# Down products of an encoder block by seven quarter products, with casting and adding transfers for their weights

## The chip, the cores and the metric

The kernel runs on one core of one Trainium2 chip. The metric is the device time of one execution in microseconds (us), as the median of several runs. The profile is that of one further execution. Engines are named as the profile names them: PE (TensorE, matmul), DVE (VectorE), ACT (ScalarE), POOL (GpSimd), SP (SyncE, which issues most transfers here).

## The reference, cut to what matters

One layer over 512 tokens of width 1024: a half-step SwiGLU (FFN1), a mixing part (convolution and gated linear attention), a second half-step SwiGLU (FFN2), a gated input embedding, a final norm. Everything is float32. The change is in the two SwiGLUs:

```python
D_MODEL = 1024; SEQ = 512; D_FF = 2816
def _swiglu(x, w_in, w_out):
    gate, up = jnp.split(x @ w_in, 2, axis=-1)
    return (jax.nn.silu(gate) * up) @ w_out

h = h + 0.5 * _swiglu(_rmsnorm(h, ffn1_norm[i]), ffn1_w_in[i], ffn1_w_out[i])
...
h = h + 0.5 * _swiglu(_rmsnorm(h, ffn2_norm[i]), ffn2_w_in[i], ffn2_w_out[i])
```

## The kernel before

**Number format.** Each float32 operand is split into a high part (a rounding copy to fp32r, on ACT: `high`, `split`) and a low part (operand minus high part, on DVE: `low`). A product is then three matmuls: high by high, low by high, high by low. A weight tile is 128 x 1024 (512 KB), so its split is one ACT cast and one DVE subtraction of 1024 elements per partition. `added` makes the low part without DVE: ACT writes minus the source (rounded) into it, and a POOL transfer adds the source.

**Gate and up.** The 2816 hidden columns are 22 blocks of 128, taken two at a time: 11 pairs. Most pairs are computed by seven quarter products (a Strassen-Winograd scheme) called m1 to m7, each of 24 matmuls with 256 moving columns. The weights' sums s1 to s4 are made by DVE (`s12`, `s3_`, `s4_`); the activations' t1 to t4 once per FFN. Some early pairs are "plain": eight units h0 to h7 of twelve 512-column matmuls. FFN1 has pairs 1 and 2 plain, FFN2 pair 1. After its products, a pair's results pass PSUM, an ACT copy (`snap`, into `sq` or `u2`), DVE additions and scalings (`plus`, `times_row`, `gated`) and an ACT Silu, and become the activations `m`; `act_parts` splits these into `actH` and `actL`.

**Down.** `CUTS` collects blocks into groups of four (the last of two). `second` computes a group as four pieces (two column halves e, two token halves th). A piece of a four-block group is 24 matmuls of 512 columns in two PSUM banks of its own; DVE then adds each bank, scaled, to the running sum `hall` (a SCALAR_TENSOR_TENSOR, called an eviction here). So a group takes 96 matmuls and 8 evictions. Its weights come as four raw 512 KB tiles, cast by ACT and subtracted by DVE.

**Order.** `drive` walks a list of units. A unit has jobs that are issued some units ahead (`AHEAD = 4`; fetches 7 or 9), then what the unit before left over (`left`, for instance the Silu), then its matmuls and evictions. `Ordered` makes PE, DVE and ACT run strictly in the order in which the instructions were issued, so an instruction that waits holds up all that stands behind it on its engine. A pair i runs m6, m7, m5 of pair i, m1 and m2 of pair i+1, m4, m3 of pair i, with pieces of the down product after m2 and after m3. Transfers issued by SP wait in SP's queue for a free buffer; `raw` has 6 buffers for weight tiles and `sm` two for sums.

Of the kernel before, what the change touches and what calls it, by code (L numbers as in the profile page):

```python
# [29 lines left out]
D_PLE = 256  # L30
EPS = 1e-6
HALF = SEQ // 2
CUTS = ((0, 4), (4, 8), (8, 12), (12, 16), (16, 20), (20, 22))


# [27 lines left out]
def block_kernel(ctx: ExitStack, tc: tile.TileContext, a: dict, out: bass.AP):  # L63
# [16 lines left out]
    def nm(s):  # L80
        uid[0] += 1
        return f"{s}_{uid[0]}"

    NA = 41
    NCV = 4

    def bt(dt=F32, s="a"):
        return big.tile([P, SEQ], dt, tag="A", bufs=NA, name=nm(s))

# [79 lines left out]
        return hi, lo  # L169

    def raw(nk, ncol):
        return wp.tile([P, 1024], F32, tag="raw", bufs=6, name=nm("wr"))[:, :nk * ncol].rearrange(
            "p (k c) -> p k c", k=nk)

    def fetch(r3, src, k0, nk, c0, ncol):
# [210 lines left out]
    class Left:  # L386
# [12 lines left out]
            dve.tensor_tensor(out=out, in0=x, in1=y, op=op)  # L399

        def tile(self):
            return wp.tile([P, 1024], F32, tag="sm", bufs=2, name=nm("sm")).rearrange("p (k c) -> p k c", k=4)

        def part(self, name, engine=None):

# [9 lines left out]
        def s12(self):  # L415
            if hasattr(self, "s1"):
                return
            self.s1, self.s2 = self.tile(), self.tile()
            self.sum(self.s1, self.a21, self.a22, ALU.add)
            self.sum(self.s2, self.s1, self.a11)  # L420

        def s3_(self):
            if hasattr(self, "s3"):
# [15 lines left out]
    def h_of(t, e):  # L439
        return hall[:, t, e * SEQ:(e + 1) * SEQ]  # L440
# [187 lines left out]
        for f in left:  # L628
            f()

    def ffn(w_in, w_out, x, nxt, given, first, rs_of, rsb, hooks, plain):


        got = {}
# [40 lines left out]
        def gated(p, s, u, i):  # L675
            if not hasattr(p, "m"):
                p.m = tmp("m", 2 * SEQ, bufs=1).rearrange("p (f c) -> p f c", f=2)
            dve.tensor_tensor(out=p.m[:, :, i * HALF:(i + 1) * HALF], in0=two(u), in1=two(s), op=ALU.mult)

        def act_parts(p):  # L680
            c = [c for c, (f0, f1) in enumerate(CUTS) if f0 <= p.f < f1][0]
            to = cvt if c % 2 == 0 and p.f == CUTS[c][0] else bt
            p.acts = [split(p.m[:, f, :], "act", to) for f in range(2)]
# [14 lines left out]

        def m6(p):
            mul(p.x, p.part("s2"), x.op["t2"], False, False)  # L700
            p.u2 = snap(p.x, "u2", bufs=1)

        def m7(p):
            p.w = bank()
# [41 lines left out]
        def unit(kind, i):  # L746
            p = pairs[i]

            def go(run):
                left = run(p)  # L750
                hooks.get((kind, i), lambda *_: None)()
                return left

            if kind[0] == "h":
                j = int(kind[1])
                part, run = (f"a{1 + j // 4}{1 + j % 2}", plain_unit(j)) if j % 4 < 2 else (None, plain_unit(j))
                if part:
                    return [(AHEAD, lambda: p.part(part)), (9, lambda: p.fetch(part))], lambda: go(run)
            else:
                part, run = USES[kind]  # L760
            before = [(AHEAD + (kind == 'm5'), lambda: p.part(part))] if part else []
            if kind in ("m1", "m2"):
                before.append((7, lambda: p.fetch(part)))
            elif kind == "m6":
                before += [(9, lambda: p.fetch("a21", "a22")), (6, p.s12)]
            elif kind in ("m7", "m3"):
                before.append((6, p.s3_ if kind == "m7" else p.s4_))

            return before, lambda: go(run)

        def second(cut):

            f0, f1 = cut
            kn = f1 - f0
            last = f1 == CUTS[-1][1]

# [33 lines left out]
                units.insert(3, ([], lambda: nxt.half(0)))  # L810
            return units

        units, had = [], set()
# [18 lines left out]
        for i in range(start, npair):  # L832
            add("m6", i)
# [12 lines left out]
            due = due[2:]  # L846
            if i in cut_of and i < end:
                due += second(cut_of[i])
        units += due + second(CUTS[-1])

        p0 = pairs[0]
# [26 lines left out]
    hooks = sums_hooks(xb, ("t2", "t3", "t1", "t4"), (("h5", 1), ("h7", 1), ("h3", 2), ("m1", 3)))  # L878
# [589 lines left out]
    def quarter(to, k, e, tag="raw", bufs=6):  # L1468
# [47 lines left out]
        sub(q11[jp], q12[jp], q11[jp])  # L1516

    def second_sum(jp):
        t2.append(narrow("sm", 2, "sm"))
        sub(t2[jp], q11[jp], q22[jp])  # L1520

    def third_sum(jp):
# [8 lines left out]
    def todo(*fs):  # L1531
        return lambda *_: [f(*v) for f, *v in fs]

    hooks.update({("d16", 1): todo((act.activation, warm, ones, AF.Sigmoid), (quarter, q11, 0, 0), (quarter, q21, 1, 0, "sm", 2), (quarter, q12, 0, 1)),
                  ("d16", 2): todo((q_high, b11, q11, 0), (quarter, q22, 1, 1), (project_in,)),
                  ("d16", 3): todo((q_high, b11, q11, 1)),
                  ("d20", 0): todo((q_high, b21, q21, 0), (first_sum, 0), (third_sum, 0)),
# [4 lines left out]
    nxt = Turn("ple_norm", xp)  # L1542
    nxt.hg = hg
    rs2_ = mid
    ffn(ffn2_in, a["ffn2_w_out"][0], xb, nxt, wf, ((g0, u0), (g1_, u1_)), lambda: rs2_[0], mid[1], hooks, (1,))

# [256 lines left out]
```

## Time and profile before

| | us |
|---|---|
| median of 3 runs (lowest to highest) | 961.56 (959.86 to 962.09) |
| the profiled execution | 960.76 |
| its span, first to last instruction | 959.0 |
| PE busy | 943.4 |
| DVE busy | 723.6 |
| ACT busy | 472.1 |
| POOL busy | 55.9 |

Rows of a timeline are start and duration in us, engine, line, operation, output<-inputs; a bracket tells how long the engine was idle before and what released it. All recorded operations carry line 46, the recording helper, so tiles tell operations apart: `wr` raw weights, `wh` and `wl` their parts, `sm` the sums s1 and s2, `hall` an eviction, `g`, `s`, `u`, `m` the steps to the activations.

### The profile page before, as it was taken

How to read it: one execution, taken by the hardware profiler on the slowest of the kernel's cores; microseconds unless marked ns; L12 is line 12 of the kernel's file. 1: busy time of each engine (PE TensorE's matmuls, PEld its weight loads, DVE VectorE, ACT ScalarE, POOL GpSimd, SP SyncE). 2: the span in 40 equal slices, each digit the busy share in tenths (PEclk: the TensorE clock that was granted, in tenths of full speed). 3: DMA queues.
4: the chain of work that ended last, by engine and by line, in shares of the span. 5: the costliest groups of instructions: out<-in, count | busy, mean ns of one | idle time of the engine just before them, and what ended most of it. 6: DMA issues, size and time to landing. Idle time of an engine off the chain costs nothing.

```text
span 959.0 us, 14433 instructions
## 1 busy us (share of the span) xinstructions
PE 943.4 (98%) x5810; PEld 832.5 (87%) x5810; DVE 723.6 (75%) x975; ACT 472.1 (49%) x721; POOL 55.9 (6%) x71
## 2 busy tenths in 40 slices
PE   9999999999999999999999999999999999999896
PEld 7888999999999988788878889999999999998674
DVE  5776877878787666999987467777777778766796
ACT  5552544334443465463566654344433443354983
POOL 0000200000000110001210010000000000001211
PEclk9999999999999999999999999999999999999998
DMA  7541223243224493255563471432233322454643
GB/s 226 178 137 62 89 90 126 71 132 110 89 70 130 138 240 85 69 130 133 133 149 98 105 176 44 133 110 89 91 108 110 113 98 77 154 198 114 116 81 107
DMA packets 90214, 112.88 MB, mean 118 GB/s; under 512 B 5075, under 2 KB 65669, under 8 KB 90148
## 3 DMA queue, kind: packets, MB, share of 16 engines
q1 hardware_dynamic: 84260, 94.67, 31.1%
q0 software_dynamic: 5872, 17.30, 9.9%
q8 instruction: 45, 0.74, 0.3%
q14 instruction: 21, 0.17, 0.1%
q10 hardware_dynamic: 16, 0.00, 0.0%
HBM read 93.61 MB, written 2.10 MB: 100 GB/s over the span
## 4 chain that ended last, share of the span: by engine, by line
PE 95%; ACT 2%; DVE 1%; DMA 0%; issue 0%; POOL 0%; POOLq 0%; SPq 0%; ACTq 0%; DVEq 0%
PE ps L46 94%; PE ax L46 1%; ACT wh L46 1%; DMA wr<-in_ffn_w_in 0%; ACT sq L46 0%; DVE s L46 0%; DVE g L46 0%; ACT hgH L46 0%; DVE rs L46 0%; DVE y L46 0%; ACT wl L46 0%; DVE wl L46 0%; POOL rs L46 0%; ACT wq L46 0%; POOLq L1801 0%
## 5 line engine op out<-in xcount | busy, mean ns | idle before, releaser
L46 PE MATMUL ps<-hgH,wh 128*128 128x256 f32 (+1 forms) x768 | 238.9, 316 | 0.2 <-DVE wh L46 0.2
L46 PE MATMUL ps<-hgL,wh 128*128 128x256 f32 (+1 forms) x768 | 237.7, 315 | 0.0
L46 PE MATMUL ps<-hgH,wl 128*128 128x256 f32 (+1 forms) x768 | 237.3, 314 | 0.0
L46 DVE TENSOR_TENSOR wl<-wr,wh 128x1024 fp32r<-128x1024 f32 (+1 forms) x158 | 188.7, 1208 | 63.2 <-ACT wh L46 63.1
L46 ACT CAST wh<-wr 128x1024 fp32r<-128x1024 f32 (+1 forms) x172 | 176.6, 1041 | 75.3 <-PE ps L46 46.5
L46 PEld LDWEIGHTS ps<-hgH,wh 128*128 128x128 f32 x768 | 146.7, 191 | 11.3 <-issue 1.1
L46 PEld LDWEIGHTS ps<-hgL,wh 128*128 128x128 f32 x768 | 146.1, 191 | 9.6 <-DVE hgL L46 0.3
L46 PEld LDWEIGHTS ps<-hgH,wl 128*128 128x128 f32 x768 | 146.4, 191 | 8.8
L46 PE MATMUL ps<-wh,actH 128*128 128x512 f32 x352 | 137.6, 391 | 0.0
L46 PE MATMUL ps<-wh,actL 128*128 128x512 f32 x352 | 137.3, 390 | 0.0
L46 PE MATMUL ps<-wl,actH 128*128 128x512 f32 x352 | 137.0, 389 | 0.0
L46 ACT ACTIVATE s<-g 128x512 f32<-128x512 f32 x48 | 30.4, 633 | 156.3 <-DVE g L46 156.3
L46 DVE SCALAR_TENSOR_TENSOR hall<-ps,rsh,hall 128x512 f32<-128x512 f32 x96 | 71.1, 748 | 29.3 <-PE ps L46 28.3
L46 DVE SCALAR_TENSOR_TENSOR cv<-glu,cw,cv 128x502 f32<-128x502 f32 (+24 forms) x120 | 81.1, 732 | 0.6
L46 PEld LDWEIGHTS ps<-wl,actH 128*128 128x128 f32 x352 | 66.1, 188 | 14.0
L46 PEld LDWEIGHTS ps<-wh,actH 128*128 128x128 f32 x352 | 66.2, 188 | 12.9
L46 PEld LDWEIGHTS ps<-wh,actL 128*128 128x128 f32 x352 | 66.2, 188 | 12.4
L46 ACT CAST wh<-sm 128x1024 fp32r<-128x1024 f32 x38 | 39.8, 1047 | 41.4 <-DVE sm L46 35.6
L46 DVE TENSOR_TENSOR wl<-sm,wh 128x1024 fp32r<-128x1024 f32 x38 | 46.3, 1222 | 4.3 <-ACT wh L46 3.9
L46 ACT COPY sq<-ps 128x512 f32<-128x512 f32 x38 | 22.3, 587 | 54.5 <-PE ps L46 54.5
L46 DVE TENSOR_TENSOR sm<-wr,wr 128x1024 f32<-128x1024 f32 x17 | 21.0, 1236 | 28.9 <-DMA wr<-in_ffn_w_in 28.9
L46 ACT CAST actH<-m 128x512 fp32r<-128x512 f32 x44 | 25.6, 619 | 31.9 <-DVE m L46 31.9
(251 smaller groups left out, 1684.1 us busy)
## 6 DMA issues: line engine op xcount, KB each, us to landing
wr<-in_ffn_w_in SPq DMA_DIRECT2D x84, 512.0 KB
wr<-in_ffn_w_out SPq DMA_DIRECT2D x44, 512.0 KB
wr<-in_w_in SPq DMA_DIRECT2D x20, 512.0 KB
wl<-wr POOLq DMA_DIRECT2D x15, 512.0 KB, 5.4
wr<-in_w_out SPq DMA_DIRECT2D x8, 512.0 KB
wq<-in_ple_w_gate SPq DMA_DIRECT2D x8, 512.0 KB
wl<-wq POOLq DMA_DIRECT2D x8, 512.0 KB, 4.6
wa<-wr POOLq DMA_DIRECT2D x12, 256.0 KB, 6.6
```

The lines of the kernel that those rows point to most:

```text
L46: inst = call(*args, **kwargs)
```

## The change

It makes four groups per FFN (blocks 4 to 20, `Q1` and `Q2`) by a new `second_quarters`; the first and the last group keep the four pieces. The two layers of the short description are the two FFNs. FFN1's pair 2 is done by m1 to m7 and no longer plain.

The activations of a group are held as quarters a11, a12, a21, a22 (two blocks by 256 tokens), its weights as b11, b12, b21, b22 (two blocks by 512 columns). Seven products, called q0 to q6 here in their order (j = 0 to 6), replace the four pieces:

| | operands | PSUM banks |
|---|---|---|
| q0 | a12 by b21 | y |
| q1 | a11 by b11 | x |
| q2 | s2 by t2 | x, added |
| q3 | s1 by t1 | x, added |
| q4 | s4 by b22 | x, added |
| q5 | s3 by t3 | w |
| q6 | a22 by t4 | w, added |

Each has 12 matmuls of 512 columns into two banks, and each is followed by two evictions of what the banks then hold. Products q1 to q4 add into the same two banks that are evicted in between, q6 into those of q5. All of b21, b11 and b22 as used by q0, q1 and q4 come straight from the input array by a casting POOL transfer (`ask`); their low parts by ACT (minus the high part) and an adding POOL transfer (`rest`). The four tiles for t1 to t4 are also loaded raw, summed by DVE, and split by `added`. DVE also makes the activations' s1 to s4, and `act_split` splits seven operands of 128 x 512 where `act_parts` split four.

```diff
-    NA = 41
+    NA = 38
+    NRAW = 10
...
+        def act_split(g, name):
+            hi, lo = two(bt(F32R, name + "H")), two(bt(F32R, name + "L"))
+            act.copy(hi, g[name])
+            sub(lo, g[name], hi.bitcast(F32))
+            g[name + "p"] = hi, lo
...
+            def ask(name, k, e):
+                w[name] = [wp.tile([P, 1024], F32R, tag=t, bufs=6, name=nm(t)).rearrange("p (k c) -> p k c", k=2)
+                           for t in ("wh", "wl")]
+                pool.dma_start(out=w[name][0], in_=src(k, e))
+            def rest(name, k, e):
+                hi, lo = w[name]
+                act.mul(lo, hi.bitcast(F32), -1.0)
+                pool.dma_start(out=lo, in_=src(k, e).bitcast(F32R), accum_op=ALU.add)
...
+            def product(key, x, y, first, last, th, e, j):
+                def run():
+                    if first:
+                        ps[key] = [bank(), bank()]
+                    wh, wl = w.pop(y)
+                    xh, xl = g.pop(x + "p")
+                    for i in range(2):
+                        ts, o = slice(i * P, (i + 1) * P), ps[key][i]
+                        for k in range(2):
+                            pe.matmul(o, xh[:, k, ts], wh[:, k], start=(first and k == 0), stop=False, skip_group_check=True)
+                            pe.matmul(o, xl[:, k, ts], wh[:, k], start=False, stop=False, skip_group_check=True)
+                            pe.matmul(o, xh[:, k, ts], wl[:, k], start=False, stop=(last and k == 1), skip_group_check=True)
+                        t = 2 * th + i
+                        h = h_of(t, e)
+                        dve.scalar_tensor_tensor(out=h, in0=o, scalar=got["rsh"][:, t:t + 1], in1=h,
+                                                 op0=ALU.mult, op1=ALU.add)
+                    hooks.get((f"d{f0}", {1: 1, 3: 2, 5: 3}.get(j)), lambda *_: None)()
+                    return []
+                return run
+            def direct(name, k, e):
+                return [(AHEAD + 2, lambda: ask(name, k, e)), (AHEAD, lambda: rest(name, k, e))]
+            jobs = [direct("b21", 1, 0) + left(("a12", None)),
+                    direct("b11d", 0, 0) + left(("a11", None)),
+                    [(AHEAD + 3, lambda: (get("b11", 0, 0), get("b12", 0, 1), get("b22", 1, 1))),
+                     (AHEAD + 2, lambda: sums("t1")), (AHEAD + 1, lambda: sums("t3", "t2")),
+                     (AHEAD, lambda: make("t2", "b22"))] + left((None, s3), ("s2", s2)),
+                    [(AHEAD, lambda: make("t1", "b11"))] + left(("s1", s1)),
+                    direct("b22d", 1, 1) + left(("s4", s4)),
+                    [(AHEAD, lambda: make("t3", "b12"))] + left(("s3", None)),
+                    [(AHEAD + 3, lambda: get("b21", 1, 0)), (AHEAD + 1, lambda: sums("t4")),
+                     (AHEAD, lambda: make("t4", "b21"))] + left(("a22", None))]
...
-        for i in range(start, npair):
+        quota = {}
+        for i in range(start, npair):
+            if i not in quota:
+                quota[i], quota[i + 1] = (len(due) + 1) // 2, len(due) // 2
+            at = {0: (), 1: "b", 2: "bd", 3: "abd", 4: "abcd"}[min(quota[i], 4)]
             add("m6", i)
             add("m7", i)
+            place("a")
             add("m5", i)
-            if i == end:
-                units += due[:1]
-                due = due[1:]
-            else:
-                add("m1", i + 1)
+            add("m1", i + 1)
             add("m2", i + 1)
-            units += due[:1]
+            place("b")
             add("m4", i)
+            place("c")
             add("m3", i)
-            units += due[1:2]
-            due = due[2:]
+            place("d")
...
-        (ps0[:2], ps0[2:]), lambda: rs1[0], lambda: spread(rs1[0]), hooks, (1, 2))
+        (ps0[:2], ps0[2:]), lambda: rs1[0], lambda: spread(rs1[0]), hooks, (1,), Q1)
```

`left(...)` puts an operand's sum and split two units ahead of its product. With the quotas, a group's products stand over two pairs. In the first pair: m6 m7 q0 m5 m1 m2 q1 m4 q2 m3 q3. In the second: m6 m7 q4 m5 m1 m2 q5 m4 m3 q6. The fourth group comes due at the last pair, which has no next pair: m6 m7 q0 m5 q1 m4 q2 m3 q3 q4 q5 q6, and then the pieces of the last two blocks. The two sums buffers `sm` are given up; sums and raw tiles share ten `raw` buffers. Work of the next stage that was hooked to pieces 1, 2 and 3 of the group at block 16 is hooked to q1, q3 and q5 now.

More of the change, by code (lines that the diff above doesn't have):

```diff
@@ L629, in drive, with ffn @@
             f()
-    def ffn(w_in, w_out, x, nxt, given, first, rs_of, rsb, hooks, plain):
+    def ffn(w_in, w_out, x, nxt, given, first, rs_of, rsb, hooks, plain, quarters):
         got = {}
@@ L675, in gated @@
         def gated(p, s, u, i):
+            if p.f - p.f % 4 in quarters:
+                g = groups.setdefault(p.f - p.f % 4, {})
+                m = g[f"a{i + 1}{1 + p.f // 2 % 2}"] = two(bt(s="m"))
+                dve.tensor_tensor(out=m, in0=two(u), in1=two(s), op=ALU.mult)
+                return
             if not hasattr(p, "m"):
@@ L811, in second, with second_quarters, src, get @@
             return units
+        def second_quarters(f0):
+            raws, w, g, ps = {}, {}, groups.setdefault(f0, {}), {}
+            def src(k, e):
+                return w_out[(f0 + 2 * k) * P:(f0 + 2 * k + 2) * P, e * SEQ:(e + 1) * SEQ].rearrange("(k p) c -> p k c", p=P)
+            def get(name, k, e):
+                raws[name] = raw(2, SEQ)
+                nc.sync.dma_start(out=raws[name], in_=src(k, e))
+            def ask(name, k, e):
[6 more added lines that the diff above has]
+                pool.dma_start(out=lo, in_=src(k, e).bitcast(F32R), accum_op=ALU.add)
+            def sums(*names):
+                for t, out_, x, y in (("t1", "b11", "b12", "b11"), ("t3", "b12", "b22", "b12"),
+                                      ("t2", "b22", "b22", "b11"), ("t4", "b21", "b21", "b22")):
+                    if t in names:
+                        sub(raws[out_], raws[x], raws[y])
+            def make(name, of):
+                w[name] = added(high(raws[of]))[:2]
+            def left(*todo):
+                def run():
+                    for name, sum_ in todo:
+                        if sum_:
+                            sum_()
+                        if name:
+                            act_split(g, name)
+                return [(2, run)]
+            def s3():
+                sub(g["a11"], g["a11"], g["a21"])
+                g["s3"] = g["a11"]
+            def s2():
+                g["s2"] = two(bt(s="s2"))
+                sub(g["s2"], g["a22"], g["s3"])
+            def s1():
+                dve.tensor_tensor(out=g["a21"], in0=g["a21"], in1=g["a22"], op=ALU.add)
+                g["s1"] = g["a21"]
+            def s4():
+                sub(g["a12"], g["a12"], g["s2"])
+                g["s4"] = g["a12"]
+            def product(key, x, y, first, last, th, e, j):
+                def run():
+                    if first:
[27 more added lines that the diff above has]
+                     (AHEAD, lambda: make("t4", "b21"))] + left(("a22", None))]
+            runs = [product(*v, j) for j, v in enumerate((
[4 rows of a table added]
+            return list(zip(jobs, runs))
@@ L1518, in second_sum @@
     def second_sum(jp):
[L1519 removed]
+        t2.append(narrow("raw", NRAW, "sm"))
         sub(t2[jp], q11[jp], q22[jp])
```

29 lines of the change are left out of this document (21 added, 8 removed), and 4 rows, old and new, of the table runs.

## The prediction

> **What bounds the kernel now.** I read the page first (busy shares, then the chain that ended last), then the matmul's pace on the timeline, then DVE's work and waits in one FFN.
>
> ```profile
> PE 943.4 (98%) x5810; PEld 832.5 (87%) x5810; DVE 723.6 (75%) x975; ACT 472.1 (49%) x721; POOL 55.9 (6%) x71
> ...
> PE 95%; ACT 2%; DVE 1%; DMA 0%; issue 0%; POOL 0%; POOLq 0%; SPq 0%; ACTq 0%; DVEq 0%
> ```
>
> PE sets the time: it is busy for 98% of the span, and the last chain runs on it for 95%. So a matmul taken away is time won, as long as nothing else makes PE wait. How much one is worth stands in the starts, not in the durations (0.28 and 0.39 us, which overlap):
>
> ```profile
> 300.03 0.28 PE L46 MATMUL ps<-hgH,wh 128*128 128x256 f32 x1
> 300.14 0.28 PE L46 MATMUL ps<-hgL,wh 128*128 128x256 f32 x1
> ...
> 305.78 0.40 PE L46 MATMUL ps<-wh,actH 128*128 128x512 f32 x1
> 306.02 0.40 PE L46 MATMUL ps<-wh,actL 128*128 128x512 f32 x1
> ...
> 311.25 0.28 PE L46 MATMUL ps<-t2H,wh 128*128 128x256 f32 x1
> ```
>
> Between 300.03 and 305.78 stand 48 matmuls of 256 columns: 0.12 us each. Between 305.78 and 311.25 stand 24 of 512 columns: 0.228 us each. A product m1 to m7 (24 narrow) takes 2.88 us, a plain unit or a quarter product q (12 wide) 2.73 us.
>
> The second question is how near DVE is to PE in the FFNs. The next rows are the window of FFN2's loop (PE, PEld, DVE, ACT and POOL busy, then clock and transfers) and DVE's waits in it:
>
> ```profile
> 592.00:842.00 250.00, 250.00 (x1742) 234.66 (x1741) 192.03 (x212) 105.41 (x132) 0.00 (x0) 1.00 0.32 105
> ```
> ```profile
> DVE wl L46 <- ACT wh L46: 29.5, 29, 2.0
> DVE sm L46 <- DMA wr<-in_ffn_w_in: 17.2, 8, 3.5
> DVE u L46 <- ACT sq L46: 8.6, 7, 1.3
> ```
>
> PE never stops in 250 us. DVE is busy for 77% of them and idles in small waits, since it works ahead. That is the cover that the change spends.
>
> **The change: what it takes from PE.** A group goes from 96 to 84 wide matmuls. Eight groups: 8 x 12 x 0.228 = 21.9 us. FFN1's pair 2 goes from 96 wide (21.9) to 168 narrow ones (20.2): 1.7 us. Together 23.5 us, if PE never waits.
>
> **What it adds to DVE.** DVE's paces, from starts of neighbours on its timeline:
>
> ```profile
> 640.49 1.22 DVE L46 TENSOR_TENSOR wl<-sm,wh 128x1024 fp32r<-128x1024 f32 x1
> 641.62 0.69 DVE L46 TENSOR_TENSOR g<-ps,sq 128x512 f32<-128x512 f32 x1
> 642.35 0.69 DVE L46 TENSOR_TENSOR g<-g,bc 128x512 f32<-128x512 f32 x1
> 642.95 0.75 DVE L46 SCALAR_TENSOR_TENSOR hall<-ps,rsh,hall 128x512 f32<-128x512 f32 x1
> ...
> 650.47 0.68 DVE L46 TENSOR_TENSOR g<-ps,bc 128x512 f32<-128x512 f32 x1
> ...
> 653.94 0.69 DVE L46 TENSOR_TENSOR m<-u,s 128x512 f32<-128x512 f32 x1
> 654.54 1.54 DVE L46 SCALAR_TENSOR_TENSOR hall<-ps,rsh,hall 128x512 f32<-128x512 f32 x2
> 656.00 1.28 DVE L46 TENSOR_TENSOR actL<-m,actH 128x512 fp32r<-128x512 f32 x2
> ...
> 664.58 0.69 DVE L46 TENSOR_TENSOR u<-ps,sq 128x512 f32<-128x512 f32 x1 [1.26 <-ACT sq L46]
> 667.05 1.23 DVE L46 TENSOR_TENSOR sm<-wr,wr 128x1024 f32<-128x1024 f32 x1 [1.78 <-DMA wr<-in_ffn_w_in]
> 668.31 1.22 DVE L46 TENSOR_TENSOR sm<-sm,wr 128x1024 f32<-128x1024 f32 x1
> 669.45 1.22 DVE L46 TENSOR_TENSOR wl<-wr,wh 128x1024 fp32r<-128x1024 f32 x1
> ```
> ```profile
> 651.19 0.63 ACT L46 ACTIVATE s<-g 128x512 f32<-128x512 f32 x1 [3.22 <-DVE g L46]
> 651.73 1.03 ACT L46 CAST wh<-wr 128x1024 fp32r<-128x1024 f32 x1
> 654.66 1.15 ACT L46 CAST actH<-m 128x512 fp32r<-128x512 f32 x2 [1.89 <-DVE m L46]
> ...
> 663.96 0.59 ACT L46 COPY sq<-ps 128x512 f32<-128x512 f32 x1 [1.90 <-PE ps L46]
> ```
>
> A long operation (1024 elements) holds DVE for 1.14 us (668.31 to 669.45), for 1.26 if the next needs its result (667.05 to 668.31). A short one takes 0.61 (642.35 to 642.95), or 0.73 if the next needs it. Two evictions take 1.4 (654.54 to 656.00). A sum whose split follows at once costs a trip over ACT: sum to cast 0.72 (653.94 to 654.66), cast 0.6, so 1.33 until the low part starts. From m5's last matmul to `u` it is 0.65 (663.96 to 664.58 and a little). From `g` to the end of the Silu it is 1.35 (650.47 to 651.19, and 0.63).
>
> Over two pairs, with one group, DVE has before: 26 long, 18 short, 8 evictions, 46 us of PE's 62.2 (336 narrow and 96 wide). After: 26 long again (the four low parts saved are the four sums t1 to t4), 25 short (four sums and three more low parts), 14 evictions. That is 30.1 + 15.9 + 9.8 = 55.8 us with the dependent ones at their price, and five trips over ACT add 3.6: 59.4. PE would need 40.3 + 84 x 0.228 = 59.4. DVE has no slack left on average, and its queue is in order, so the local chains decide.
>
> **Three stalls in each two pairs.** I laid DVE's queue end to end against PE's units, in the order in which the built program issues them. Wherever DVE must wait for PE and then has more to do before PE's next need than PE has work, PE stops, every time.
>
> *Into q5.* m5 ends; `u` starts 0.65 later, since it needs the copy of m5. Behind it on DVE: `u` 0.61, two sums of weights 1.26 each, s4 of the weights 1.14, t4 1.14, a low part 1.14, the low part of the activations' s3 0.69. That is 7.9 us. PE has m1 and m2, 5.76, and one matmul of q5 that needs only the high part, 0.23. Stall 1.9 us.
>
> *Into q2.* It adds into the banks of q1, so q1's eviction must be over. From q0's end: its second eviction 0.7, t3, t2 and a low part 3.4, `u` and the low part of a11 1.2, two sums 2.5, s4 and a low part 2.3, s3 of the weights 1.14, s3 of the activations 0.73, s2 with its trip 1.33, its low part 0.61, `g` twice 1.34, q1's first eviction 0.75: 16.0 us. PE has m5, m1, m2, q1, m4: 14.25. Stall 1.8.
>
> *Into q3.* From q2's start (q1's first eviction is done): second eviction 0.67, a low part 1.14, `u` and `m` 1.34, a low part 1.14, s1 with its trip 1.33, its low part 0.61, q2's first eviction 0.75: 7.0 us. PE has q2 and m3: 5.6. Stall 1.4.
>
> The same reckoning leaves q4 (8.4 of 8.5 us) and q6 (6.8 of 8.5) just free. Sum 5.1 us: two pairs take 64.5 us instead of 62.2. Each FFN has three such cycles: 6 x 5.1 = 30.6 us.
>
> **The fourth group.** In the last pair q3 to q6 stand back to back. q4 needs the eviction of q3, and before it on DVE from q3's start: an eviction 0.67, s4 with its trip and low part 1.94, `g` and Silu 1.35, a weight cast behind the Silu on ACT 1.0 and its low part 1.14, another low part 0.61, `m` 0.61, the eviction 0.75: 8.1 us where PE has q3, 2.7. Stall 5.3; in FFN2 I take 4.8, since DVE arrives 0.6 earlier. In FFN1 the next stage's weights (eight ACT operations of some 0.6 us, twice, from the hooks at m4 and q3) stand ahead of s1's and a22's casts: I add 1.5 into q3 and 2.2 into q6, in FFN2 0.4. Sum 14 us. Before, the pieces had banks of their own, and nobody waited.
>
> **What I cost at nothing.** Loads: tiles t1 to t4 are asked for only a unit before their first use, but SP may issue as soon as a buffer is free, and with ten buffers the tile that held it was done six units (17 us) earlier or more; before, some had one or two units, the 17.2 us of waits above. If the cover is gone, these waits come back, at most 2.1 us a pair. The casting POOL transfer does not occur before. Its nearest rows:
>
> ```profile
> wl<-wr POOLq DMA_DIRECT2D x15, 512.0 KB, 5.4
> ...
> sm<-in_ple_w_gate POOLq DMA_DIRECT2D x2, 512.0 KB, 7.6
> ```
>
> At 5.4 to 7.6 us it lands in time: `rest` on ACT comes two units (5.6 us) after the issue, and behind it wait first a Silu whose result is due a product later. I take 0; the upper end is 2 us for each of 24 transfers on ACT's queue, 48 us with all of it passed on, and I let a third of it count in the range. FFN1's early part has DVE near PE's pace for ten units (about 33 us of each): 0 taken, 3 at most.
>
> [...]
>
> **Sum.** -23.5 + 30.6 + 14 = +21.1 us on the profiled execution's 960.76 us (span 959.0 and 1.8 around it): 981.9. The median of the runs shown lies 0.8 higher, so 983 us.
>
> **Rivals.**
> *All hidden.* DVE and ACT keep ahead of PE and the time falls by the whole 23.5: 938 us. For it: DVE idles for 23% now. Against it: the chains above start at PE's own ends, where being ahead is of no use.
> *Half hidden.* The stalls are half of what I work out, because paces overlap more than the starts show: -23.5 + 22 = 960 us, no change. Against it: the paces agree within 0.02 us from row to row.
> *ACT becomes a bound.* ACT's `rest` waits for the casting transfers and holds up casts and Silus, at 0.7 us or more for each of 24: 983 + 17 = 1000 us and above. For it: ACT's work grows by about 9 us a group (seven more long operations, three more casts, from 6.6 to about 16). Against it: its share stays near 55%.
>
> **Chances.** Forecast 0.64 (its own range 970 to 996); all hidden 0.08; half hidden 0.11, in which faster, same and slower get 0.05, 0.02 and 0.04; ACT a bound 0.17. Faster by over 0.2% (which this measurement can just tell) 0.13, within it 0.02, slower 0.85. The range 960 to 1003 leaves out the all-hidden case, part of the half-hidden one and the far end of ACT's.
>
> **What would show it.** Right: PE idles ahead of q2, q3 and q5 by 1 to 2 us in each cycle, released by DVE, and ahead of q4 by about 5 us at each FFN's end; two pairs take about 64.5 us; DVE's busy share is above 80%; DVE no longer waits for raw weights. Wrong: a PE without idle time in the loops (all hidden), or waits of ACT's multiply for POOL's transfers with PE idle ahead of m products too (ACT a bound). The forecast fails if the stalls in a cycle sum to under 3 us or over 8.

## The result and the profile after

The changed kernel takes 1023.85 us (median of 4 runs, 1022.18 to 1024.59) where the kernel before takes 960.71 beside it: the ratio is 1.065, interval 1.063 to 1.067. That is slower, as forecast, but by 63 us and not by 21: the time lies outside the range, 960 to 1003. The profiled execution has a span of 1022.1 us. One run of a later kernel (the late `u`), at 1304 us and a mean granted clock of 0.656, is left out of that kernel's figure. The page (busy times, then the chain that ended last):

```profile
PE 952.0 (93%) x5786; PEld 834.1 (82%) x5786; DVE 802.6 (79%) x1089; ACT 541.4 (53%) x807; POOL 129.2 (13%) x151
...
PE 67%; DVE 13%; issue 7%; ACT 6%; DMA 6%; POOL 0%; POOLq 0%; SPq 0%; DVEq 0%; ACTq 0%
```

TensorE is no longer the whole chain: a third of it is DVE, ACT, transfers and issue. And TensorE is busy for 952 us where 943.4 less 23.5 would be 920: its matmuls have become slower. What TensorE waits for (total us, times, longest):

```profile
PE ps L48 <- DVE hall L48: 20.1, 7, 3.2
PE ps L48 <- DVE s3L L48: 11.6, 6, 1.9
PE ps L48 <- DMA wl<-in_ffn_w_out: 6.2, 4, 2.8
PE ps L48 <- ACT actH L48: 5.4, 1, 5.4
PE ps L48 <- ACT wa L48: 4.9, 1, 4.9
PE ps L48 <- ACT sq L48: 4.7, 1, 4.7
```

Six gaps into q2 (`hall`, q1's eviction), six into q5 (`s3L`), one into q4 at each FFN's end (put down to `actH` and `wa`; the eviction of q3 ended just before): all where the forecast has them. The six gaps of 1.4 us into q3 that it also has are not there. New are the waits for the adding transfer and one gap of 4.7 us in FFN1's pair 2. The matmuls behind a gap into q2, on TensorE's timeline, and the clock there (window, busy times of PE, PEld, DVE, ACT and POOL, granted clock, transfers):

```profile
157.00 0.76 PE L48 MATMUL ps<-wh,s2H 128*128 128x512 f32 x1 [3.03 <-DVE hall L48]
157.57 0.63 PE L48 MATMUL ps<-wh,s2L 128*128 128x512 f32 x1
157.99 0.63 PE L48 MATMUL ps<-wl,s2H 128*128 128x512 f32 x1
```
```profile
157.00:159.00 2.00, 2.00 (x5) 1.61 (x6) 1.69 (x3) 1.74 (x2) 0.00 (x0) 0.50 1.02 352
159.00:161.00 2.00, 2.00 (x8) 1.58 (x7) 1.97 (x4) 0.00 (x0) 0.00 (x0) 0.72 0.33 97
161.00:163.00 2.00, 2.00 (x17) 1.92 (x17) 1.26 (x3) 0.79 (x2) 0.00 (x0) 1.00 0.63 208
```

For 3 us behind the gap a matmul starts every 0.43 us, at a clock of 0.50, where it started every 0.228. The clock falls here after idle times of 3.0 us and, in three of the six gaps into q5, of 1.9 (behind the one at 186.63 it is 0.50 from 187.63 to 190.63).

Two pairs (q2 to the next q2) take 68.2 to 68.9 us, where I had 64.5:

```profile
157.00:225.45 68.45, 63.33 (x421) 58.30 (x421) 56.58 (x66) 33.89 (x43) 9.39 (x10) 0.95 0.68 170
225.45:293.93 68.48, 63.33 (x421) 58.26 (x421) 56.57 (x66) 33.90 (x43) 9.39 (x10) 0.95 0.67 168
715.88:784.07 68.19, 62.04 (x421) 57.23 (x421) 56.11 (x66) 33.79 (x43) 9.35 (x10) 0.97 0.68 171
784.07:852.95 68.88, 62.36 (x421) 57.14 (x421) 56.29 (x66) 33.80 (x43) 9.36 (x10) 0.98 0.67 170
```

Read by the starts of the transposes of `hall` that end each FFN, FFN1 ends 34.6 us later (355.62 before, 390.22 after), FFN2 takes 28.0 us more (546.60 to 886.86 before, 581.22 to 949.51 after), and the part between them (from FFN1's last transposes, at 365.55 and 400.15) loses nothing: 181.05 and 181.07.

### The profile page after: what moved, and what is told of

Its sections match the earlier page's. It is cut to its first block, busy times and chain, and to the rows that moved or that the text cites. A ratio compares the mean times of both kernels' runs of the same rounds, so it can differ in the third digit from the quotient of the medians.

```text
span 1022.1 us, 14828 instructions
## 1 busy us (share of the span) xinstructions
PE 952.0 (93%) x5786; PEld 834.1 (82%) x5786; DVE 802.6 (79%) x1089; ACT 541.4 (53%) x807; POOL 129.2 (13%) x151
## 4 chain that ended last, share of the span: by engine, by line
PE 67%; DVE 13%; issue 7%; ACT 6%; DMA 6%; POOL 0%; POOLq 0%; SPq 0%; DVEq 0%; ACTq 0%
PE ps L48 67%; DMA wl<-in_ffn_w_out 4%; DVE sm L48 3%; DVE wl L48 2%; DVE wr L48 2%; DVE g L48 1%; ACT wh L48 1%; DMA wl<-wr 1%; ACT sq L48 1%; ACT wl L48 1%; DVE s L48 1%; DMA wr<-in_ffn_w_out 1%; DVE m L48 1%; ACT wa L48 1%; DVE hall L48 1%
## 5 line engine op out<-in xcount | busy, mean ns | idle before, releaser
L48 DVE TENSOR_TENSOR wl<-wr,wh 128x1024 fp32r<-128x1024 f32 (+1 forms) x127 | 151.9, 1204 | 43.9 <-ACT wh L48 43.2
L48 DVE SCALAR_TENSOR_TENSOR hall<-ps,rsh,hall 128x512 f32<-128x512 f32 x144 | 104.5, 746 | 28.7 <-PE ps L48 28.3
L48 POOL DMA_DIRECT2D wl<-wr x47 | 41.5, 883 | 293.1 <-ACT wl L48 221.9
L48 DVE TENSOR_TENSOR wr<-wr,wr 128x1024 f32<-128x1024 f32 x50 | 60.9, 1218 | 0.3
L48 POOL DMA_DIRECT2D wl<-in_ffn_w_out x24 | 29.2, 1215 | 172.6 <-DVE hall L48 90.2
L48 ACT ACTIVATE wl<-wr 128x1024 fp32r<-128x1024 f32 x47 | 49.8, 1059 | 0.0
L48 POOL DMA_DIRECT2D wh<-in_ffn_w_out x24 | 17.7, 736 | 245.9 <-PE ps L48 235.8
L48 PE MATMUL ps<-t1H,wh 128*128 128x256 f32 x144 | 41.5, 288 | 4.7 <-ACT sq L48 4.7
L48 PE MATMUL ps<-t1L,wh 128*128 128x256 f32 x144 | 41.3, 287 | 0.0
L48 PE MATMUL ps<-t1H,wl 128*128 128x256 f32 x144 | 41.3, 287 | 0.0
```

What stands on the lines that cost most here:

```text
L48: inst = call(*args, **kwargs)
```

## The experiments

The kernel before took 960.7 to 961.5 us beside these runs; "against" means against the changed kernel's 1023.85. FFN1's pair 2 (pairs count from 0) is "the third pair" in some of the expectations. Three theories stood at the start. A: gaps from DVE's queue, each with a stretch of half clock. B: the half clock has another cause. C: DVE's whole work sets the cycle.

**Keep TensorE busy in the gaps.**
```diff
+ n = {4: 36}.get(j) if f0 == 16 else {2: 24, 5: 14}.get(j)
+ if n:
+     warm_up(n)
```


> This kernel computes what the changed one does and issues dummy transposes of the identity (24 ahead of q2, 14 ahead of q5 in the three cycles of each FFN, 36 ahead of q4 in the last group) into the spare bank, so that TensorE is busy while it waits. The waits on DVE stay as they are. Theory A (TensorE's clock falls to half because TensorE stood idle, and stays there for some 3 us after each gap): the matmuls after these 14 gaps start every 0.23 us instead of 0.43, which is worth about 1.4 us each, 20 us in all: 1004 us (1000 to 1010), and the mean granted clock goes up from 0.971 to about 0.99. Rival B (the slow stretches come from the loads or from the new order of products, not from the idle time): 1022 to 1026 us, and the slow stretches stay.

Measured: 1023.39 us (1.066, 1.062 to 1.069), mean clock 0.988. TensorE's waits:

```profile
157.66 0.47 PE L48 MATMUL ps<-wh,s2H 128*128 128x512 f32 x1 [0.41 <-DVE hall L48]
...
165.01 0.47 PE L48 MATMUL ps<-wh,s1H 128*128 128x512 f32 x1 [1.48 <-DVE hall L48]
...
206.28 0.50 PE L48 MATMUL ps<-wl,a12H 128*128 128x512 f32 x1 [1.47 <-DMA wl<-in_ffn_w_out]
```
```profile
157.60:160.00 2.40, 2.34 (x10) 1.98 (x11) 2.09 (x3) 1.81 (x2) 0.00 (x0) 1.00 0.98 315
```

B falls: with the dummies the clock is 1.00 behind the gap. But A's 20 us fall too, for time that TensorE wins is lost at the next wait: q3 now waits 1.48 us for q2's eviction, the stall of 1.4 that I had forecast and that the slow matmuls had covered, and q0 waits 1.47 for its weights. The half clock stands in place of other waits.

**s3's split a unit earlier**, ahead of `u`: `left(("s3", None))` becomes `left(("s3", None), far=3)`.

> This kernel issues the split of s3 (for q5) three units ahead instead of two, so that its low part stands on DVE ahead of u of m5 and of the five long operations behind it. Theory A (the stall is set by the order of DVE's queue): the gap of 1.94 us into q5 goes in all six cycles, with the 1.4 us of half clock behind each: 6 x 3.3 = 20 us less than the changed kernel's 1023.9, 1004 us (1000 to 1008). Rival C (DVE is full, so that what is won at one place is lost at the next): the gaps into q2 or q3 grow by as much, 1018 to 1026 us.

Measured: 1030.03 us (1.071, 1.067 to 1.074). The gap into q5 is gone, and this one is new, ahead of q6:

```profile
197.06 0.79 PE L48 MATMUL ps<-wl,a22H 128*128 128x512 f32 x1 [2.67 <-DMA wl<-wr]
```

The sum t4 stands behind `u` as well, and its cast and adding transfer come late instead. A cycle takes 69.15 us.

**Other places for the products** (the sum s4 is made with s2, too).
```diff
- quota[i], quota[i + 1] = (len(due) + 1) // 2, len(due) // 2
+ quota[i], quota[i + 1] = len(due) // 2, (len(due) + 1) // 2
```


> This kernel puts three quarter products into the first pair of a cycle and four into the second (q0, q1, q2 at a, b, d; q3 to q6 at a, b, c, d), so that m4 and m3, not m4 alone, lie between q1 and q2, and one unit more ahead of q5; the sum s4 is made right after s2, which frees a buffer that the order needs. Theory A: the gap into q2 falls from 3.15 to about 0.3 us, the gap into q5 goes, and with them two stretches at half clock per cycle: 6 x (5.1 + 2 x 1.4) = 47 us at most; the last group gets worse, since q3 now follows q2 at once (2 to 3 us an FFN): 980 to 988 us. Rival C (DVE is full): gaps come back at other places and the time stays above 1005 us.

Measured: 1025.84 us (1.067, 1.065 to 1.069), where A had 980 to 988. A cycle takes 68.2 us (221.08 to 289.31), with the gaps into q1 and q6 now:

```profile
221.08 0.50 PE L48 MATMUL ps<-wh,a11L 128*128 128x512 f32 x1 [3.20 <-DVE a11L L48]
...
265.57 0.47 PE L48 MATMUL ps<-wh,a22H 128*128 128x512 f32 x1 [2.37 <-DVE hall L48]
```

Three arrangements, one cycle: C looked right.

**The fourth group plain**: `Q1` and `Q2` become `(4, 8, 12)`.

> This kernel leaves the fourth group (blocks 16 to 19) of both FFNs with the plain down product of the kernel before. Theory A: the gaps of the last group go (8.8 us in FFN1: 2.8, 1.1, 4.9; 7.4 in FFN2: 2.0, 5.4) and with them five stretches at half clock (7 us); the 12 more wide matmuls of each group cost 2 x 2.7 us: 1023.9 - 16 - 7 + 5.5 = 1006 us (1002 to 1011). Rival (the end of an FFN is bound by the last pair's own chain, whatever stands there): 1020 us or more.

Measured: 1009.56 us (1.051, 1.048 to 1.054), 14.3 less against, where 18 were expected. The gaps at the ends are gone. In FFN2 9 us are won there (from the last gap into q5 to the transposes, 66.9 to 57.9), but a wait of 3.6 us for an adding transfer is new in its third cycle.

**Less work for DVE**, a test of C: the low parts of a11 and a12 are not made, and their products read the high parts in their place. Here and in the next runs on low parts, a11 and a12 are the weights of m1 and m2, not the activations' quarters of the same names.

> This kernel leaves out the low parts of the weights a11 and a12 in all narrow pairs (the product reads the high part in their place, with as many matmuls), so that DVE has four long operations, 4.7 us, less in each cycle, and nothing else changes. Three arrangements so far (the dummies, s3 early, the other places) left the cycle at 68.2 to 69.2 us. Theory C (the cycle is as long as DVE's in-order queue laid end to end, its waits for ACT and PE included, so that each operation counts): the cycle falls by about 4.7 to near 64 us, 28 us in six cycles and 2 to 4 in the early part: 990 to 998 us. Theory A (only the operations that stand in the three chains ahead of q2, q3 and q5 count): at most two of the four, 8 to 14 us: 1010 to 1016.

Measured: 1017.14 us (1.058, 1.054 to 1.061). Between two q2 (217.96 and 287.01):

```profile
217.96:287.01 69.05, 63.55 (x421) 58.43 (x421) 51.77 (x62) 33.90 (x43) 9.36 (x10) 0.94 0.67 169
```

DVE has 4.8 us less to do and the cycle is no shorter. C falls, as does each account by DVE's busy share; nor do two of these four operations count in a cycle, as A's 1010 to 1016 would need. The 7 us are won in FFN1's pair 2, whose gap of 4.7 us is gone. In the cycle DVE only waits longer, ahead of q0's eviction:

```profile
199.24 0.75 DVE L48 SCALAR_TENSOR_TENSOR hall<-ps,rsh,hall 128x512 f32<-128x512 f32 x1 [4.10 <-PE ps L48]
```

**Sums a unit ahead of their splits**: `left(("s1", s1))` becomes `[(3, s1)] + left(("s1", None))`, and so for s2 and s4.

> This kernel issues the sums s3 and s2, s1 and s4 one unit ahead of their splits, so that DVE does not stand idle while ACT casts a sum that was just made (0.7 us, three times a cycle). Theory C: the cycle falls by about 2 us, 12 to 14 us in all: 1010 us (1007 to 1014). If the time that DVE wins is lost again in its waits for PE, 1020 us or more.

Measured: 1011.41 us (1.052, 1.049 to 1.055), in the expected range, but by other parts: the cycles fall by 0.5 to 1.4 us where 2 were expected (67.1 in FFN1), and the rest is won ahead of the first cycle and at the ends. The trips over ACT stand in a chain: into q2 the gap is 2.4 instead of 3.15.

**The same low parts by adding transfers**: `p.add_part(part)` for m1 and m2 in place of `p.part(part)`.

> This kernel makes the same four low parts (a11 and a12 of both pairs) by ACT's multiply and an adding POOL transfer in place of DVE's subtraction: the result is the reference's. Theory C: as in the kernel without them, near 64 us a cycle, 990 to 1000 us. Rival D (the adding transfers are themselves the next bound; TensorE already waits for them up to 2.8 us at a time): TensorE's waits for wl by DMA grow from 7 us to more than 20, and the time stays above 1010.

Measured: 1018.14 us (1.060, 1.057 to 1.063): the same as without them, so again only FFN1's pair 2. TensorE's waits for `wl` grow from 7 to 11 us, not to 20.

**FFN1's pair 2 alone**: `Q1 = Q2 = ()`.

> This kernel keeps of the change only FFN1's third pair by quarters (and the smaller buffers); all down products are plain. My sum for this part: 1.7 us less of matmuls. The trace of the changed kernel shows one gap of 4.7 us there, with a slow stretch of 1.4 behind it: 960.8 - 1.7 + 6.1 = 965 us (963 to 967). If the gap comes from the quarter products' work in the queues: 959 to 960.

Measured: 966.56 us (1.005, 1.004 to 1.007). This part (with the changed buffers), for which I had taken 1.7 us off, costs 5.

**`u` later on DVE** (theory E: two chains, each from a point where DVE waits for TensorE):
```diff
- p.u = plus(p.w, snap(p.x, "sq", bufs=3), "u1")
+ half = snap(p.x, "sq", bufs=3)
+ def late_u():
+     p.u = plus(p.w, half, "u1")
+ return [late_u]
```


> Only one operation moves on DVE: u of m5 (which waits for the end of m5's matmuls) is issued behind the weight and split operations of the next unit instead of ahead of them. Theory E (leaving out four long operations moved nothing in the cycle, so the cycle is not set by DVE's sum of work but by two chains that begin where DVE waits for TensorE: from m5's end over u to q5, and from q0's end over its eviction to q1's eviction and q2): the first chain loses its start, the gap into q5 (1.94 us) goes with the half clock behind it, and the cycle falls by 2 to 3.5 us; the gap into q2 stays near 3.2: 1003 to 1012 us. Rival C (DVE's sum of work): no change, 1020 or more.

Measured: 1020.2 us as the mean of three runs, 1018.4 to 1023.6 (1.062, 1.059 to 1.064); E's 1003 to 1012 is missed. The gap into q5 goes; the one into q2 grows to 3.7, and q0 waits 1.3 to 2.7 us for its transfer.

**Evictions of q0, q4, q6 later too**: `return [lambda: None, evict]`.

> As with the late u, and the evictions of q0, q4 and q6, whose banks nobody needs soon, are issued behind the operations of the next unit and its run. Theory E: the second chain loses its start too (DVE has 4 us of idle time ahead of q0's end that it can now fill), the gap into q2 falls below 1 us, and the cycle goes from 68.4 to 61 to 64 us: 985 to 998 us, with the gaps of the last groups left. Rival C: 1015 or more.

Measured: 1025.88 us (1.067, 1.064 to 1.069). E fails as put: the gap into q2 stays at 3.7. Here the trace shows why. ACT's rows, then DVE's:

```profile
283.04 0.59 ACT L48 COPY sq<-ps 128x512 f32<-128x512 f32 x1 [8.27 <-PE ps L48]
283.52 1.05 ACT L48 CAST wh<-wr 128x1024 fp32r<-128x1024 f32 x1
284.46 1.06 ACT L48 ACTIVATE wl<-wr 128x1024 fp32r<-128x1024 f32 x1
285.42 0.61 ACT L48 CAST a11H<-m 128x512 fp32r<-128x512 f32 x1
```
```profile
280.17 0.75 DVE L48 SCALAR_TENSOR_TENSOR hall<-ps,rsh,hall 128x512 f32<-128x512 f32 x1 [1.24 <-PE ps L48]
286.06 0.69 DVE L48 TENSOR_TENSOR a11L<-m,a11H 128x512 fp32r<-128x512 f32 x1 [5.15 <-ACT a11H L48]
```

DVE is free at 280.9 and then stands for 5 us, waiting for the cast of a11. That cast needs nothing new; but it stands on ACT behind the copy of m5, and ACT waits 8.3 us for m5's end. So the chain into q2 begins at m5's end, in ACT's queue (theory F).

**All repairs so far together** (late `u` and evictions, s3 and the sums earlier, fourth group plain, and `add_part` for m1 and m2 of FFN1's pair 2):

> All of it together: late u and evictions, s3's split three units ahead, sums a unit ahead of their splits, the fourth group plain, and in FFN1's third pair the low parts of a11 and a12 by adding transfers (their leaving out closed the gap of 4.7 us there). Theory E: a cycle of 60 to 62 us (TensorE's own work is 59.4), no gaps at the ends and none early: 960.8 - 1.7 - 6 x (62.2 - 61) = 952 us (944 to 962). Rival: DVE, busy for 56.5 us of each cycle, now becomes the bound itself, with its waits for ACT: cycles above 64 us and 970 or more.

Measured: 992.03 us (1.032, 1.029 to 1.035), its runs from 985 to 998, far from E's 952. The gap into q2 is still 2.8 to 3.0 in each cycle.

**a11's split a unit earlier, alone**: `left(("a11", None), far=3)`, ahead of m5's copy on ACT.

> One thing moves: the split of a11 (for q1) is issued three units ahead, so that ACT's cast a11H stands ahead of its copy of m5 (sq), which waits for m5's end. Theory F (the chain into q2 begins at m5's end through ACT's queue: sq, two casts, a11H, then a11L and all that follows on DVE): the chain from m5's end to q2 becomes 0.65 + 0.61 + 3.7 + 1.14 + 1.14 + 2 + 0.6 + 1.3 + 0.75 = 11.9 us where TensorE has 11.4, so the gap into q2 falls from 3.15 to about 0.5 us and the cycle from 68.4 to about 66; the gap into q5 stays: 1008 us (1003 to 1013). Theory E as it was put (the chain begins at q0's end): the gap into q2 stays near 3 us, 1020 or more.

Measured: 1015.15 us (1.057, 1.055 to 1.058), 9 us less against where 16 were expected. The gap into q2 falls from 3.15 to 2.03, not to 0.5:

```profile
223.70 0.47 PE L48 MATMUL ps<-wh,s2H 128*128 128x512 f32 x1 [2.03 <-DVE hall L48]
...
231.00 0.47 PE L48 MATMUL ps<-wh,s1H 128*128 128x512 f32 x1 [1.45 <-DVE hall L48]
```

What remains is the chain that I had forecast, from q0's end, with its 1.8 us: DVE now works without a wait for a11 from q0's second eviction (207.45) to q1's, 16.25 us to q2's start. Two chains lead into q2, and the longer one hid mine.

**The combination with a11's split.**

> The combination of the run before (late u and evictions, s3 and the sums earlier, fourth group plain, two adding transfers in FFN1's third pair), and a11's split three units ahead. Theory F: the gap into q2, 2.97 us in each cycle there, falls below 0.5, and the half clock behind it goes: 6 x 4 us less than 992, 968 us (955 to 975), with the waits for the adding transfers of w_out left. If the gap into q2 stays at 2 us or more, theory F is wrong: above 980.

Measured: 971.43 us (1.010, 1.008 to 1.012), 21 us less than without that one edit, where it won 9 alone. The gaps into q2 are 0.85 us and less; F stands. Waits of 1.8 to 3.0 us for the adding transfers of `in_ffn_w_out` are left.

**And the direct operands by plain loads:**
```diff
- return [(AHEAD + 2, lambda: ask(name, k, e)), (AHEAD, lambda: rest(name, k, e))]
+ def go():
+     w[name] = added(high(raws.pop(name + "r")))[:2]
+ return [(AHEAD + 2, lambda: get(name + "r", k, e)), (AHEAD, go)]
```


> As the last one, and the direct operands b21, b11 and b22 come by a plain load, ACT's cast and multiply and an adding transfer inside the chip, in place of a casting transfer and an adding transfer from DRAM: POOL's queue no longer stops at a casting transfer that waits for a free buffer, with an adding transfer behind it. Theory F with the transfers as the second cost: TensorE's waits for wl by DMA go, 10 us less than the kernel with them: 958 us (945 to 966). Rival: ACT's three more casts and the buffers held longer cost as much: within 3 us of it.

> The changed kernel with only the direct operands b21, b11 and b22 by a plain load, cast, multiply and an adding transfer inside the chip. Rival G (the casting and adding transfers are what the loss comes from): 1000 us or less. Theory F: only TensorE's waits for wl of w_out go, 6 us in all with up to as much half clock behind: 1012 to 1022 us, and the gaps into q2 and q5 stay at 3.1 and 1.9 us.

Measured: 960.28 us for the combination (ratio 0.9994, 0.9985 to 1.0004), 1025.93 for the edit alone on the changed kernel (1.068, 1.066 to 1.069). So the transfers cost 11 us where nothing else makes TensorE wait. The edit alone falls outside F's 1012 to 1022. TensorE's 6.2 us of waits for `wl` of `in_ffn_w_out` are gone in its trace, but a larger one is new, ahead of q4 at FFN2's end, where ACT waits for a load and DVE 9.5 us for ACT's cast behind it (TensorE's row, then ACT's):

```profile
932.44 0.77 PE L48 MATMUL ps<-wh,s4H 128*128 128x512 f32 x1 [12.82 <-DVE hall L48]
```
```profile
928.13 1.04 ACT L48 CAST wh<-wr 128x1024 fp32r<-128x1024 f32 x1 [7.75 <-DMA wr<-in_ffn_w_out]
```

In the changed kernel this gap is 5.4. So its total does not tell what the transfers cost; rival G, with 1000 us or less, is wrong all the same, since the gaps into q2 and q5 stay.

**What is left of the gain.** FFN1's pair 2 plain again, then the places of the third experiment on top of that:

> The last combination with FFN1's third pair plain again, as in the kernel before, and so with two groups by quarters in FFN1 (blocks 8 to 15) and three in FFN2. Both pieces are read from traces: in the run with only the third pair by quarters, FFN1's eleventh pair begins 4.5 us later than before; in the last combination a cycle takes about 61 us for 62.2 before. Theory F: 5 cycles at 1 to 1.2 us less than before, nothing lost elsewhere: 956 us (953 to 959), below both kernels. If the gain of a cycle is eaten by what lies around it: 959 to 962.

> As the last one, with three products in the first pair of a cycle and four in the second, which takes q2 behind m3 and q3 into the next pair: the gaps of 0.25 and 0.69 us into q2 and q3 go. Theory F (with the chains from m5's end cut, the places are free to choose): a cycle of 60 us, 951 us (948 to 956). If q1's split or q5's eviction is now late, as in the first run with these places (gaps of 3.2 and 2.4 us): 962 or more.

Measured: 960.62 us (0.9995, 0.9986 to 1.0004) and 995.18 (1.036, 1.033 to 1.038), where F had 956 and 951. No version beats the kernel before. Two pairs with one group, in the first of the two, stand at 61.0 us where the kernel before has 62.16; the same stretch of both, the repaired kernel first:

```profile
186.93:249.09 62.16, 61.14 (x427) 57.15 (x426) 57.50 (x68) 36.81 (x46) 6.02 (x7) 1.00 0.69 176
```
```profile
186.93:249.09 62.16, 62.16 (x433) 58.33 (x432) 47.64 (x53) 26.01 (x33) 0.00 (x0) 1.00 0.32 102
```

TensorE has 1.0 us of waits in them (0.33 into q2, 0.69 into q3), and DVE and the transfers are loaded to 57.5 of 62.2 us and to 0.69. With the other places q6 waits 4.2 to 5.3 us for q5's eviction.

**The two chains alone** (late `u`, a11's split earlier):

> The changed kernel with two moves alone, each of which takes one chain off m5's end: u behind the next unit's operations (DVE) and a11's split three units ahead (ACT). Theory F: with both, the gap into q5 goes and the gap into q2 falls to 1 to 1.5 us (the casts of sums still cost their 0.7 us each), the cycle goes from 68.4 to about 64 us, and the ends, the early gap and the waits for transfers stay: 997 us (990 to 1004). If the chains are not what sets the cycle, more than 1010.

Measured: 1007.02 us (1.048, 1.046 to 1.050), 17 us less against, where the two edits alone won 4 and 9; short of the 27 expected. The gap into q2 is 1.3 to 2.4 us. It is q0's chain again, from the start of its second eviction (DVE) to q2 (TensorE):

```profile
206.33 0.75 DVE L48 SCALAR_TENSOR_TENSOR hall<-ps,rsh,hall 128x512 f32<-128x512 f32 x1 [1.44 <-PE ps L48]
```
```profile
222.58 0.47 PE L48 MATMUL ps<-wh,s2H 128*128 128x512 f32 x1 [1.31 <-DVE hall L48]
```

That is 16.25 us; the forecast laid the same work end to end and had 16.0.

## Why the prediction was right and wrong

**Right.** The direction, and the mechanism: TensorE stops where a chain on DVE begins at TensorE's own end. Into q5 I had 1.9 us, measured 1.94 in each of six cycles. Into q3 1.4, measured 1.43 to 1.54 as soon as the matmuls ahead of it run at full clock (1.48 with the dummies, at 165.01). Into q4 at the ends 5.3 and 4.8, measured 4.9 and 5.4. DVE waits 1.3 us in all for raw weights. The two rivals with less loss were wrong. DVE's share is 79%, just under the 80% that I had named.

**Luck.** TensorE is idle for 5.1 us of a cycle in FFN1 (68.45 less 63.33), just the 5.1 of the forecast. But the parts differ: the stall into q2 is 1.35 longer, the one into q3 isn't there, and the cycle still comes out 3.9 us longer, since TensorE is busy for 63.3 us where I had 59.4, with part of its matmuls at half clock.

**The step that failed: "Into q2 [...] From q0's end".** There are two chains into q2, and I laid out only DVE's. The other goes through ACT. These are ACT's and DVE's rows in the changed kernel:

```profile
210.96 0.59 ACT L48 COPY sq<-ps 128x512 f32<-128x512 f32 x1 [4.68 <-PE ps L48]
211.44 1.05 ACT L48 CAST wh<-wr 128x1024 fp32r<-128x1024 f32 x1
212.39 1.06 ACT L48 ACTIVATE wl<-wr 128x1024 fp32r<-128x1024 f32 x1
213.35 0.61 ACT L48 CAST a11H<-m 128x512 fp32r<-128x512 f32 x1
```
```profile
213.99 0.69 DVE L48 TENSOR_TENSOR a11L<-m,a11H 128x512 fp32r<-128x512 f32 x1 [1.02 <-ACT a11H L48]
214.60 1.22 DVE L48 TENSOR_TENSOR sm<-wr,wr 128x1024 f32<-128x1024 f32 x1
...
222.62 0.69 DVE L48 TENSOR_TENSOR s2L<-s,s2H 128x512 fp32r<-128x512 f32 x1 [0.69 <-ACT s2H L48]
...
224.56 1.40 DVE L48 SCALAR_TENSOR_TENSOR hall<-ps,rsh,hall 128x512 f32<-128x512 f32 x2
```
```profile
225.45 0.77 PE L48 MATMUL ps<-wh,s2H 128*128 128x512 f32 x1 [3.15 <-DVE hall L48]
```

From m5's end (the copy at 210.96) to q2 at 225.45 it is 14.5 us, and TensorE has m1, m2, q1 and m4, 11.4: hence 3.15 instead of 1.8. Counted from q0's second eviction (208.09) it is 17.36 us where I had 16.0: the wait of 1.02 for a11's cast, and 0.3 on the work itself. The cast of a11 alone, taken ahead of that copy, brings the gap to 2.0.

**Terms left out.** The half clock: 1.5 to 2.5 us behind each gap into q2 and about 1.9 behind three of the six into q5, where the sum of the forecast has nothing. Behind the two stalls into q4 it takes 1.5 and 2.0 (q4 takes 4.3 and 4.7 us for 2.75). It is not a term to add everywhere: behind q2 it covers the stall into q3, and with the dummies the time stays the same. Behind the other gaps into q5 waits for adding transfers stand in its place: 1.0 and 1.4 us in FFN2's first two cycles, 2.8 ahead of the fourth group in FFN1.

The cycle from 157.00 to 225.45, then:

| us | forecast | measured |
|---|---|---|
| TensorE's own work | 59.4 | 59.5 (14 products m of 2.875 and 7 products q of 2.75, as they run where nothing waits) |
| into q5 | 1.9 | 1.94 |
| into q2 | 1.8 | 3.15 |
| into q3, or the half clock that covers it | 1.4 | 1.5 (q2 takes 4.28, 157.00 to 161.28) |
| half clock behind q5, or the wait for a transfer | 0 | 1.9 (q5 takes 6.55 with its wait, 184.30 to 190.85) |
| sum | 64.5 | 68.0, of 68.45 |

The rest of 0.45 us is in delays of up to 0.2 us at the starts of single products. Six cycles at 3.9 more than forecast are 23 us of the 41.5 by which the two FFNs missed the forecast (34.6 and 28.0 against 21.1). The chain over ACT is 1.35 of the 3.9, 8 us in all; the larger part is what I had put at nothing.

**The other 18 us.** FFN1's pair 2 was taken at a gain of 1.7 ("FFN1's early part [...] 0 taken, 3 at most") and costs 5 by itself. The ends of the FFNs lose some 12 us more than forecast: in the traces FFN1 is 34.6 longer, of which 3 x 6.2 are cycles and 4.5 pair 2 (its eleventh pair begins at 315.70 instead of 311.25 where pair 2 is changed alone), which leaves 11.5 for its end where the forecast has 6.3 (9.0 of stalls less 2.7 of matmuls); FFN2's end has 9.4 for 2.5. There the fourth group's q0 waits 2.8 and 2.0 us for an adding transfer, and the half clock follows four of the five gaps. That FFN1's three gaps there sum to 8.8 us, near my 9.0, is luck again: none stands ahead of q6, where I had 2.2.

**What I cost at nothing.** The casting transfers: ACT was not held up as the rival had it (its multiplies wait 1.5 us in all for casting transfers, in two waits), so that rival is wrong in its mechanism, though its time, 1000 us and above, is the one that came. But POOL's queue is: a casting transfer that waits for a free buffer holds up the adding one behind it. ACT's and POOL's rows in the run with late evictions:

```profile
263.58 1.05 ACT L48 ACTIVATE wl<-wh 128x1024 fp32r<-128x1024 f32 x1
```
```profile
265.19 0.72 POOL L48 DMA_DIRECT2D wh<-in_ffn_w_out  x1 [7.31 <-PE ps L48]
265.90 1.24 POOL L48 DMA_DIRECT2D wl<-in_ffn_w_out  x1
```

The adding transfer's multiply was done at 264.63, and it left POOL at 265.90, behind the casting one: 1.3 us late, where TensorE then waits 2.1 us for it (at 276.06; the next one leaves at 274.13). Without these transfers the time is 11 us less once the other waits are gone; how much of that is the order in POOL's queue, and how much the transfers' own time, is not shown.

The 23.5 us saved on TensorE were there in matmuls (59.5 us a cycle for 62.2), but with all repairs a cycle gains 1.1 of the 2.8 that I had, and the time only comes back to that of the kernel before. In the version with pair 2 plain, the traces show where that gain goes. Its two cycles in FFN1 take 61.0 and 61.1 us for 62.16 before, 2.2 us in all; but the late `u` makes TensorE wait in FFN1's first pair of products m (1.7 us later from there on), and FFN1's end takes 0.6 longer:

```profile
120.08 0.39 PE L48 MATMUL ps<-hgH,wh 128*128 128x256 f32 x1 [1.43 <-DVE u L48]
...
723.77 0.50 PE L48 MATMUL ps<-wl,a12H 128*128 128x512 f32 x1 [1.18 <-DMA wl<-wr]
```

FFN2's three cycles take 60.9, 62.1 and 61.8, the last two with waits of 1.2 and 0.5 us for adding transfers, and its end takes 0.6 longer. Together FFN1 ends 0.1 us later than before and FFN2 takes 1.0 less: nothing that the runs could tell from no change.

## What to carry to other kernels

Lay out the chains into a stall on every in-order engine that feeds it: a copy on ACT that waits for a matmul's end holds up a cast that was ready long before, and DVE with it (here the cast of a11: in the run with late evictions ACT waited 8.27 us for m5's end, and DVE 5.15 for that cast). Busy shares say little there; leaving out 4.8 us of DVE's work per cycle made no cycle shorter, since DVE then waited longer at the next point where it needs TensorE. And where several waits stand one behind the other, a repair tried alone can show a small loss (s3's split, the late evictions, the plain loads: 2 to 6 us more), and the others won 45 us in sum (the plain fourth group, the sums, a11's split, the adding transfers, the late `u`), while all together won 63: judge a repair by whether its gap closes and which wait takes its place, not by the total.

## What the runs showed of the hardware

How long TensorE must stand idle for the granted clock to fall to half was not fixed. In windows of 0.5 us over the changed kernel's trace it stayed at 1.00 behind idle times of 0.97, 1.01, 1.15 and 1.65 us (at 823.75, 764.04, 364.12 and 966.86) and fell to 0.50 behind all eleven of 1.98 to 5.40. Behind the six gaps into q5, 1.93 or 1.94 each, it fell three times (at 186.63, 255.03 and 882.60) and stayed three times. The other runs, too, have it both ways: half after 1.65 (the run with a11's split alone, at 959.88), 2.04 and 2.43 (the two chains alone, at 289.49 and 202.90), full after 2.43 (the first gap into q2 in the run with a11's split alone) and even 3.48 (the run with low parts by adding transfers, at 828.76). The stretches behind 1.65, 2.43 and 3.48, in this order:

```profile
959.90:961.90 2.00, 2.00 (x5) 1.58 (x6) 1.29 (x3) 1.97 (x4) 0.68 (x1) 0.55 0.00 0
```
```profile
156.40:158.40 2.00, 2.00 (x9) 1.67 (x10) 1.68 (x3) 1.70 (x2) 0.00 (x0) 1.00 1.04 359
```
```profile
828.80:830.80 2.00, 2.00 (x9) 1.65 (x10) 0.75 (x1) 0.00 (x0) 0.00 (x0) 1.00 1.07 210
```

Where it fell, it could begin up to 1.5 us after TensorE had started again (the two chains alone: from 202.90 to 204.40 a matmul starts every 0.23 to 0.34 us, then every 0.41 to 0.43). In the changed kernel's trace, up to 940 us, it lasted 3.4 us twelve times and 6.8 us twice (from 293.25 and from 928.2). Why one idle time goes both ways, no run here shows.
